# A fused hybrid decoder layer on one core: seven-product groups with one weight sum made by an adding transfer, two made by one VectorE instruction, and five more such groups

## The chip, the cores and the metric

The kernel runs on one core of a Trainium2 chip, as one launch. The metric is device time in microseconds (us), the median of a few runs. Engines are named as in the profile: PE is TensorE (PEld its weight loads), DVE is VectorE, ACT is ScalarE, POOL is GpSimd, SP is SyncE. A "queue" of an engine is the order in which it starts its own instructions, transfers that it issues included.

## The reference

One decoder layer on 256 tokens of width 2048, all in float32: a norm, one wide projection, a state-space scan and an attention (with dilations) side by side, an output projection, a norm, a two-layer MLP with a squared ReLU, a norm. What matters here are the matrix products with W_out (4096 x 2048), W_up (2048 x 8192) and W_down (8192 x 2048):

```python
y_mix = jnp.concatenate([y_ssm, y_att], axis=-1)
mix = jnp.einsum('bse,ed->bsd', y_mix, w_out)
h = h + rmsnorm(mix, norm_mix_post[i])
u = rmsnorm(h, norm_mlp_pre[i])
hdn = jax.nn.relu(jnp.einsum('bsd,df->bsf', u, w_up))
ff = jnp.einsum('bsf,fd->bsd', hdn * hdn, w_down)
h = h + rmsnorm(ff, norm_mlp_post[i])
```

## The kernel before, in words

**Precision by splitting.** The matmuls take a 32-bit type of reduced precision, so each float32 operand is split into two parts (`split`, L138 and L139): ACT copies it into the reduced type (`hi`), and DVE subtracts that from the original (`lo`). A product is then three matmuls: hi by hi, hi by lo, lo by hi. Weights are split as they come in, activations once they exist. In the profile a weight tile is `raw` (or `raw_p`, from another pool), its parts `hi` and `lo` (or `hi_p`, `lo_p`).

**Groups.** From the sixth pair of row blocks of W_out on, the work is a list of groups (`Group`). A group is 256 rows by 1024 columns of a weight matrix, 1 MB: two row blocks of 128 (a with index 0, 1 for the row block and b for the second half of the columns), each a `raw` tile of 128 x 2 x 512. It is multiplied by the matching 256 features of both halves of the tokens. There are four results of 128 tokens by 512 columns, held in four PSUM banks over all the groups of a unit (a unit is a half of W_out, an eighth of W_up, a half of W_down).

A **plain** group (`plain`, L815 to L817) makes eight block products of three matmuls: 24 matmuls of 512 columns. A **seven-product** group (`seven`, L827 to L829) uses the Strassen-Winograd scheme for 2 x 2 blocks: seven block products, 21 matmuls. It needs sums of weight blocks and of activation blocks first, and has four more PSUM banks (`more`), which `combine` adds together after the last seven-product group of a unit (L877 to L881), and `final` joins to the plain ones (L885). The weights' sums are made by `add` (L793, four DVE instructions of 128 x 512, one of them written over a half of raw[0]); three of the results lie in one tile `xr`, which is split into `xh` and `xl` (one tile each, 128 x 1536). The activations' sums are made by `sums` (L707 to L715: tile `uu`, split into `q` or `m` tiles); sums of W_out's and W_up's activations are kept for the next unit, those of W_down are made for each group, since there the activations are the hidden columns. Those are also split again for every two groups (`ready`, q<-m).

**Order.** From here on the program's order is written by hand (a manual schedule): each engine runs its instructions as they were recorded. `run` walks through a unit; before the matmuls of group i, `advance(i + 2)` records work ahead: the fetch of group i + 4 (two 512 KB transfers on SP's queue, L784), the splits of group i + 2 (`divide`), the weight sums and the activation sums of group i + 3. Six raw tiles (three groups) and six pairs of hi and lo (three groups) are in turn, one `xr`, one `xh` and one `xl`. A fetch waits until the tile of the group three earlier is split; a split waits until TensorE is done with the group three earlier. In a seven-product group raw[1] is fetched and split first.

POOL's queue holds in this part only a few transfers of 1 MB (L910: norm weights, L950: x or the stored h, L991: h to memory) and a few small operations.

Of the kernel before, what the change touches and what calls it, by code (L numbers as in the profile page):

```python
# [14 lines left out]
ALU = mybir.AluOpType  # L15

P = 128
# [54 lines left out]
def hymba_layer(ctx: ExitStack, tc: tile.TileContext, x, norm_mix_pre, w_in, conv_w, conv_b, dt_bias, a_log,  # L72
# [604 lines left out]
    class Mix:  # L677
# [32 lines left out]
        def sums(self):  # L710
            if self.k not in self.kept:
                a, c = self.source(), quarters(strip())
                nc.vector.tensor_tensor(c[:, 0:2], a[:, 0::3], a[:, 1:2].to_broadcast([P, 2, P]), op=ALU.subtract)
                nc.vector.tensor_tensor(c[:, 2], a[:, 0], c[:, 1], op=ALU.add)
                nc.vector.tensor_tensor(c[:, 3], a[:, 2], c[:, 2], op=ALU.subtract)  # L715
                d = self.tile()
                split(d[:, 0], d[:, 1], c)
                self.kept[self.k] = d
            self.d = self.kept[self.k]
# [54 lines left out]
    class Group:  # L774
# [3 lines left out]
        def fetch(self):  # L778
            self.raw = [raw_tile() for _ in range(KB)]
            self.hl = [None, None]  # L780
            cs = slice(self.n * NB, (self.n + 2) * NB)
            for j in (1, 0) if self.by_seven else (0, 1):
                k = self.acts.k * KB + j
                nc.sync.dma_start(self.raw[j].rearrange("p b n -> p (b n)"), self.src[k * P:(k + 1) * P, cs])  # L784

        def add(self):
            if not self.by_seven:
                return
            self.x = pp.tile([P, 3, NB], F32, name="xr")
            (a0, b0), (a1, b1) = ((r[:, 0], r[:, 1]) for r in self.raw)  # L790
            e0, s, t4 = (self.x[:, i] for i in range(3))
            for dst, p, q in ((e0, a0, b0), (s, b0, b1), (b0, e0, b1), (t4, b0, a1)):
                nc.vector.tensor_tensor(dst, p, q, op=ALU.add)  # L793

# [4 lines left out]
        def divide(self):  # L799
            self.acts.ready()  # L800
            for j in (1, 0) if self.by_seven else (0, 1):
                if self.hl[j] is None:
                    self.part(j, hl_tiles())
            if self.by_seven:
                self.xhl = aside()
                split(*self.xhl, self.x)
# [12 lines left out]
        def seven(self, acc, more, first, last):  # L819
            block, summed = self.acts.block, self.acts.summed  # L820
            (a0, e1), (a1, b1) = ([[v[:, b] for v in hl] for b in range(2)] for hl in self.hl)
            e0, s, t4 = ([v[:, i] for v in self.xhl] for i in range(3))
            for dst, (a_h, a_l), (hi, lo), own in (
                    (acc[0], block(1, 0), a1, False), (acc[1], summed(3), b1, False),
                    (more[0], block(0, 0), a0, True), (more[2], summed(2), e1, True),
                    (more[1], summed(1), e0, True), (more[3], summed(0), s, True), (acc[2], block(1, 1), t4, False)):
                nc.tensor.matmul(dst, a_h, hi, start=own and first, stop=False)  # L827
                nc.tensor.matmul(dst, a_h, lo, start=False, stop=False)  # L828
                nc.tensor.matmul(dst, a_l, hi, start=False, stop=own and last)  # L829
# [10 lines left out]

    at = {"fetch": 0, "add": 0, "sums": 0, "divide": 0}

    def advance(to, sums=True):

        with tc.high_priority(offset=AHEAD):
            for what, last in (("fetch", to + 2), ("divide", to), ("add", to + 1), ("sums", to + 1)):
                while at[what] <= min(last, len(groups) - 1):
                    g = groups[at[what]]
                    if what == "divide" and at["add"] == at["divide"]:
                        g.add()  # L850
                        at["add"] += 1
                    if what == "sums":
# [20 lines left out]
    def combined(r):  # L873

        def combine(more):
            u_ = strip()
            nc.scalar.activation(r[0, 0], more[0], AF.Copy)  # L877
            nc.vector.tensor_tensor(u_, r[0, 0], more[2], op=ALU.subtract)
            nc.vector.tensor_tensor(r[1, 0], more[3], u_, op=ALU.add)
# [4 lines left out]
    def final(r, acc, t, b):  # L884
        nc.vector.tensor_tensor(r[t, b], acc[b + 2 * t], r[t, b], op=ALU.subtract if b else ALU.add)  # L885

# [21 lines left out]
    def load_wpost(pool, src):  # L908
# [3 lines left out]

    wo0 = plan(w_out, 0, Mix, order_of(range(EARLY, 16), (6, 9, 12)))
    wo1 = plan(w_out, 2, Mix, order_of((0, 1, 6, 2, 4, 3, 9, 5, 12, 7, 8, 10, 11, 13, 14, 15), (6, 4, 9, 12, 8)))
    up = [plan(w_up, 2 * n, Pre,
               order_of(range(8), ()) if n == 0 else
               order_of((0, 1, 3, 2, 5, 4, 7, 6), (3, 5, 7)) if n < 7 else
               order_of((0, 1, 3, 2, 5, 4, 6, 7), (3, 5))) for n in range(8)]
    down = [plan(w_down, 2 * n, Hidden, order_of(range(32), range(4, 27, 3) if n == 0 else range(3, 25, 3)))
            for n in range(2)]  # L920
# [161 lines left out]
    for n in range(8):  # L1082
# [5 lines left out]
        else:  # L1088
            hooks.update({i: Pre(k).sums for i, k in ((0, 3), (1, 5), (2, 7))})
        run(unit, acc, more, combined(r), hooks, started=n == 0)  # L1090
# [65 lines left out]
```

## Time and profile before

| | |
|---|---|
| median of three runs | 1495.16 us (1495.01 to 1495.42) |
| profiled execution, its own time | 1493.86 us |
| its span, first to last instruction | 1491.8 us |
| granted TensorE clock, mean | 0.995 |
| busy: PE, PEld, DVE, ACT, POOL | 1471.1, 1242.0, 1157.7, 845.2, 54.1 us |
| matmuls | 7229 |
| read from memory | 281.78 MB, 192 GB/s over the span |
| seven-product groups (xh splits counted) | 44 |

The kernel runs W_in with its scan and attention until some 603 us, W_out until 789, W_up until 1143 and W_down to the end. Busy shares are means over these stages. In a row of the timeline the first number is the start and the second the duration in us; then come engine, line, operation, the tiles written and read, and in brackets how long the engine sat idle before it and what ended that. Instructions of one engine overlap a little (the next starts before the last has fully ended), so what an instruction costs its engine is the distance from its start to the next one's.

### The profile page before, as it was taken

Reading aid. Unit: us, or ns where it says so; the run is one execution under the profiler, and the core shown is the slowest. Engines: PE = TensorE matmul, PEld = TensorE weight load, DVE = VectorE, ACT = ScalarE, POOL = GpSimd, SP = SyncE. Lnnn points to the kernel's source line nnn. Section 1 sums busy time; section 2 is a strip of 40 time slices with the busy share of each in tenths; the row PEclk is TensorE's granted clock in tenths of the full one; section 3 lists DMA queues with packets and bytes.
Section 4 is the critical chain, followed back from the end, with each engine's and each line's share of the span. In section 5 each row is a group of like instructions: output and inputs, shape, how many; then the busy total and the mean of one; then the engine's idle time right before and its main releaser. Section 6 shows DMA issues by size and latency. Waiting matters only on the chain. (4 is left out here: it accounts for less than half of the span.)

```text
span 1491.8 us, 19561 instructions
## 1 busy us (share of the span) xinstructions
PE 1471.1 (99%) x7229; PEld 1242.0 (83%) x7229; DVE 1157.7 (78%) x1609; ACT 845.2 (57%) x1138; POOL 54.1 (4%) x77
## 2 busy tenths in 40 slices
PE   9999999999999999999997999999999999999997
PEld 8888888888888888878885888888888888888886
DVE  6988897886555555597987778888887899779995
ACT  7574565455545454554556565676665665656462
POOL 0002100220000000000001000000000000000000
PEclk9999999999999999999999999999999999999998
DMA  7666666555656555555674555655555556657652
GB/s 270 203 201 181 182 185 186 182 169 169 175 167 182 169 170 176 190 169 205 247 238 176 187 176 211 211 186 187 197 182 193 199 196 216 221 186 259 219 188 96
DMA packets 108751, 287.28 MB, mean 193 GB/s; under 512 B 11392, under 2 KB 14320, under 8 KB 107632
## 3 DMA queue, kind: packets, MB, share of 16 engines
q1 hardware_dynamic: 103632, 272.37, 56.2%
q0 software_dynamic: 1152, 8.39, 1.6%
q10 hardware_dynamic: 3872, 5.28, 1.1%
q8 instruction: 56, 0.92, 0.3%
q14 instruction: 39, 0.32, 0.1%
HBM read 281.78 MB, written 4.23 MB: 192 GB/s over the span
## 5 line engine op out<-in xcount | busy, mean ns | idle before, releaser
L139 DVE TENSOR_TENSOR lo<-raw,hi 128x1024 fp32r<-128x1024 f32 (+1 forms) x367 | 447.9, 1224 | 181.6 <-ACT hi L138 180.8
L138 ACT ACTIVATE hi<-raw 128x1024 fp32r<-128x1024 f32 (+1 forms) x367 | 383.7, 1050 | 278.1 <-PE acc L221 108.5
L221 PE MATMUL acc<-q,hi 128*128 128x512 f32 x1024 | 283.3, 402 | 0.6 <-DVE q L141 0.6
L221 PEld LDWEIGHTS acc<-q,hi 128*128 128x128 f32 x1024 | 178.8, 189 | 27.3 <-DVE q L141 0.8
L817 PE MATMUL acc<-hi,q 128*128 128x512 f32 x472 | 183.7, 389 | 0.0
L815 PE MATMUL acc<-hi,q 128*128 128x512 f32 x472 | 183.6, 389 | 0.0
L816 PE MATMUL acc<-lo,q 128*128 128x512 f32 x472 | 183.6, 389 | 0.0
L224 PEld LDWEIGHTS acc<-q,lo 128*128 128x128 f32 x1024 | 152.9, 189 | 19.2
L224 PE MATMUL acc<-q,lo 128*128 128x256 f32 x1024 | 157.8, 281 | 0.0
L139 DVE TENSOR_TENSOR lo<-raw_p,hi 128x1024 fp32r<-128x1024 f32 x95 | 115.8, 1219 | 16.3 <-ACT hi L138 16.2
L138 ACT ACTIVATE hi<-raw_p 128x1024 fp32r<-128x1024 f32 x95 | 99.7, 1050 | 33.3 <-DVE raw_p L793 15.0
L816 PEld LDWEIGHTS acc<-lo,q 128*128 128x128 f32 x472 | 88.6, 188 | 18.5
L817 PEld LDWEIGHTS acc<-hi,q 128*128 128x128 f32 x472 | 88.6, 188 | 18.5
L815 PEld LDWEIGHTS acc<-hi,q 128*128 128x128 f32 x472 | 88.6, 188 | 18.3
L199 PE MATMUL acc<-hi,q 128*128 128x512 f32 x256 | 100.1, 391 | 0.0
L200 PE MATMUL acc<-lo,q 128*128 128x512 f32 x256 | 99.7, 389 | 0.0
L201 PE MATMUL acc<-hi,q 128*128 128x512 f32 x256 | 99.7, 389 | 0.0
L138 ACT ACTIVATE q<-uu 128x512 fp32r<-128x512 f32 x21 | 13.3, 632 | 132.9 <-DVE uu L715 132.9
L139 DVE TENSOR_TENSOR xl<-xr,xh 128x1536 fp32r<-128x1536 f32 x44 | 77.3, 1757 | 11.2 <-ACT xh L138 11.0
L138 ACT ACTIVATE xh<-xr 128x1536 fp32r<-128x1536 f32 x44 | 65.1, 1480 | 15.3 <-PE ps L829 7.5
L139 DVE TENSOR_TENSOR lo_p<-raw,hi_p 128x1024 fp32r<-128x1024 f32 x43 | 52.5, 1220 | 12.8 <-ACT hi_p L138 12.8
L815 PE MATMUL ps<-hi,q 128*128 128x512 f32 x152 | 59.5, 392 | 0.0
(361 smaller groups left out, 2565.3 us busy)
## 6 DMA issues: line engine op xcount, KB each, us to landing
raw<-in_w_in_dram SPq DMA_DIRECT2D x190, 512.0 KB, 3.6
raw<-in_w_up_dram SPq DMA_DIRECT2D x86, 512.0 KB, 4.5
raw<-in_w_down_dram SPq DMA_DIRECT2D x85, 512.0 KB, 5.1
raw<-in_w_out_dram SPq DMA_DIRECT2D x46, 512.0 KB, 4.0
raw_p<-in_w_down_dram SPq DMA_DIRECT2D x43, 512.0 KB, 5.1
raw_p<-in_w_up_dram SPq DMA_DIRECT2D x42, 512.0 KB, 4.6
raw_p<-in_w_out_dram SPq DMA_DIRECT2D x18, 512.0 KB, 5.1
bc<-acs_d ACTq DMA_DIRECT2D x8, 512.0 KB, 4.6
```

The lines of the kernel that those rows point to most:

```text
L138: return (nc.scalar.activation(hi, src, AF.Copy), nc.vector.tensor_tensor(lo, src, hi.bitcast(F32), op=ALU.subtract))
L139: nc.vector.tensor_tensor(lo, src, hi.bitcast(F32), op=ALU.subtract))
L199: nc.tensor.matmul(acc[t], a_h[:, r, ts], hi[:, j], start=begin, stop=False)
L200: nc.tensor.matmul(acc[t], a_h[:, r, ts], lo[:, j], start=False, stop=False)
L201: nc.tensor.matmul(acc[t], a_l[:, r, ts], hi[:, j], start=False, stop=end)
L221: nc.tensor.matmul(acc[f], hi[:, j, f * P:(f + 1) * P], u(k0 + j), start=k0 + j == 0, stop=False, skip_group_check=True)
L224: nc.tensor.matmul(acc[f][:, 0], lo[:, j, f * P:(f + 1) * P], u(k0 + j)[:, 0], start=False, stop=k0 + j == NK - 1, skip_group_check=True)
L815: nc.tensor.matmul(a, a_h, hi[:, b], start=first and j == 0, stop=False)
L816: nc.tensor.matmul(a, a_h, lo[:, b], start=False, stop=False)
L817: nc.tensor.matmul(a, a_l, hi[:, b], start=False, stop=last and j == KB - 1)
```

## The change

The seven-product groups get another form of the scheme. With a0, b0 the two halves of row block 0 and a1, b1 those of row block 1, the sum s = b0 + b1 is made by a transfer: POOL issues a third load, of the 256 KB of b1, that adds to the half of raw[0] that holds b0 (L786 of the new kernel). It has to wait until raw[0] has landed. `add` then is two DVE instructions (L793 and L794 of the new kernel): x0 = s - a0 of 128 x 512, and x1, x2 = (a1, b1) - x0 as one of 128 x 1024. It isn't a step of its own one group ahead any more, but stands in `divide` between the splits of raw[1] and raw[0]. The activations' sums and the signs in `combine` and `final` change with the scheme, at the same number and size of instructions. Two products change places in `seven`.

The groups are placed anew. W_out's first half has four seven-product groups instead of three (its groups 1, 3, 5 and 7, counted from 0; before 1, 4 and 7), its second half five as before, W_up twenty as before, at the same places in a unit but with row pair 1 in place of 5. Each half of W_down has ten instead of eight: groups 4, 7, 9, 12, 15, 17, 20, 23, 25, 28 of the first (before every third from 4 to 25) and 3, 6, 8, 11, 14, 16, 19, 22, 24, 27 of the second (before every third from 3 to 24). That makes 49 instead of 44.

```diff
--- before.py
+++ after.py
@@ -710,7 +710,7 @@
         def sums(self):
             if self.k not in self.kept:
                 a, c = self.source(), quarters(strip())
-                nc.vector.tensor_tensor(c[:, 0:2], a[:, 0::3], a[:, 1:2].to_broadcast([P, 2, P]), op=ALU.subtract)
+                nc.vector.tensor_tensor(c[:, 0:2], a[:, 1::2], a[:, 0:2], op=ALU.subtract)
                 nc.vector.tensor_tensor(c[:, 2], a[:, 0], c[:, 1], op=ALU.add)
                 nc.vector.tensor_tensor(c[:, 3], a[:, 2], c[:, 2], op=ALU.subtract)
                 d = self.tile()
@@ -782,15 +782,17 @@
             for j in (1, 0) if self.by_seven else (0, 1):
                 k = self.acts.k * KB + j
                 nc.sync.dma_start(self.raw[j].rearrange("p b n -> p (b n)"), self.src[k * P:(k + 1) * P, cs])
+            if self.by_seven:
+                nc.gpsimd.dma_start(self.raw[0][:, 1], self.src[k * P + P:(k + 2) * P, (self.n + 1) * NB:cs.stop],
+                                    accum_op=ALU.add)
 
         def add(self):
             if not self.by_seven:
                 return
             self.x = pp.tile([P, 3, NB], F32, name="xr")
-            (a0, b0), (a1, b1) = ((r[:, 0], r[:, 1]) for r in self.raw)
-            e0, s, t4 = (self.x[:, i] for i in range(3))
-            for dst, p, q in ((e0, a0, b0), (s, b0, b1), (b0, e0, b1), (t4, b0, a1)):
-                nc.vector.tensor_tensor(dst, p, q, op=ALU.add)
+            nc.vector.tensor_tensor(self.x[:, 0], self.raw[0][:, 1], self.raw[0][:, 0], op=ALU.subtract)
+            nc.vector.tensor_tensor(self.x[:, 1:3], self.raw[1], self.x[:, 0:1].to_broadcast([P, KB, NB]),
+                                    op=ALU.subtract)
 
         def part(self, j, tiles):
             self.hl[j] = tiles
@@ -801,6 +803,8 @@
             for j in (1, 0) if self.by_seven else (0, 1):
                 if self.hl[j] is None:
                     self.part(j, hl_tiles())
+                if j and self.by_seven:
+                    self.add()
             if self.by_seven:
                 self.xhl = aside()
                 split(*self.xhl, self.x)
@@ -818,12 +822,12 @@
 
         def seven(self, acc, more, first, last):
             block, summed = self.acts.block, self.acts.summed
-            (a0, e1), (a1, b1) = ([[v[:, b] for v in hl] for b in range(2)] for hl in self.hl)
-            e0, s, t4 = ([v[:, i] for v in self.xhl] for i in range(3))
+            (a0, s), (a1, b1) = ([[v[:, b] for v in hl] for b in range(2)] for hl in self.hl)
+            x0, x1, x2 = ([v[:, i] for v in self.xhl] for i in range(3))
             for dst, (a_h, a_l), (hi, lo), own in (
                     (acc[0], block(1, 0), a1, False), (acc[1], summed(3), b1, False),
-                    (more[0], block(0, 0), a0, True), (more[2], summed(2), e1, True),
-                    (more[1], summed(1), e0, True), (more[3], summed(0), s, True), (acc[2], block(1, 1), t4, False)):
+                    (more[0], block(0, 0), a0, True), (more[3], summed(0), s, True),
+                    (more[2], summed(2), x0, True), (more[1], summed(1), x2, True), (acc[2], block(1, 1), x1, False)):
                 nc.tensor.matmul(dst, a_h, hi, start=own and first, stop=False)
                 nc.tensor.matmul(dst, a_h, lo, start=False, stop=False)
                 nc.tensor.matmul(dst, a_l, hi, start=False, stop=own and last)
@@ -838,17 +842,14 @@
     def order_of(ks, by_seven):
         return [(k, k in by_seven) for k in ks]
 
-    at = {"fetch": 0, "add": 0, "sums": 0, "divide": 0}
+    at = {"fetch": 0, "sums": 0, "divide": 0}
 
     def advance(to, sums=True):
 
         with tc.high_priority(offset=AHEAD):
-            for what, last in (("fetch", to + 2), ("divide", to), ("add", to + 1), ("sums", to + 1)):
+            for what, last in (("fetch", to + 2), ("divide", to), ("sums", to + 1)):
                 while at[what] <= min(last, len(groups) - 1):
                     g = groups[at[what]]
-                    if what == "divide" and at["add"] == at["divide"]:
-                        g.add()
-                        at["add"] += 1
                     if what == "sums":
                         if g.by_seven:
                             g.acts.sums()
@@ -875,14 +876,14 @@
         def combine(more):
             u_ = strip()
             nc.scalar.activation(r[0, 0], more[0], AF.Copy)
-            nc.vector.tensor_tensor(u_, r[0, 0], more[2], op=ALU.subtract)
+            nc.vector.tensor_tensor(u_, more[2], r[0, 0], op=ALU.add)
             nc.vector.tensor_tensor(r[1, 0], more[3], u_, op=ALU.add)
             nc.vector.tensor_tensor(r[0, 1], more[1], u_, op=ALU.add)
             nc.vector.tensor_tensor(r[1, 1], more[3], r[0, 1], op=ALU.add)
         return combine
 
     def final(r, acc, t, b):
-        nc.vector.tensor_tensor(r[t, b], acc[b + 2 * t], r[t, b], op=ALU.subtract if b else ALU.add)
+        nc.vector.tensor_tensor(r[t, b], acc[b + 2 * t], r[t, b], op=ALU.add)
 
     def four():
         return {(t, b): pp.tile([P, NB], F32, name="r", bufs=4) for t in range(NT) for b in range(2)}
@@ -910,13 +911,14 @@
         nc.gpsimd.dma_start(w.rearrange("p n c -> p (n c)"), src[0].partition_broadcast(P))
         return w
 
-    wo0 = plan(w_out, 0, Mix, order_of(range(EARLY, 16), (6, 9, 12)))
+    wo0 = plan(w_out, 0, Mix, order_of((5, 6, 7, 9, 10, 8, 11, 12, 13, 14, 15), (6, 9, 8, 12)))
     wo1 = plan(w_out, 2, Mix, order_of((0, 1, 6, 2, 4, 3, 9, 5, 12, 7, 8, 10, 11, 13, 14, 15), (6, 4, 9, 12, 8)))
     up = [plan(w_up, 2 * n, Pre,
                order_of(range(8), ()) if n == 0 else
-               order_of((0, 1, 3, 2, 5, 4, 7, 6), (3, 5, 7)) if n < 7 else
-               order_of((0, 1, 3, 2, 5, 4, 6, 7), (3, 5))) for n in range(8)]
-    down = [plan(w_down, 2 * n, Hidden, order_of(range(32), range(4, 27, 3) if n == 0 else range(3, 25, 3)))
+               order_of((0, 2, 3, 4, 1, 5, 7, 6), (3, 1, 7)) if n < 7 else
+               order_of((0, 2, 3, 4, 1, 5, 6, 7), (3, 1))) for n in range(8)]
+    down = [plan(w_down, 2 * n, Hidden, order_of(range(32), (4, 7, 9, 12, 15, 17, 20, 23, 25, 28) if n == 0 else
+                     (3, 6, 8, 11, 14, 16, 19, 22, 24, 27)))
             for n in range(2)]
 
     region = tc.manual_schedule()
@@ -1086,7 +1088,7 @@
         if n:
             hooks[1] = turned
         else:
-            hooks.update({i: Pre(k).sums for i, k in ((0, 3), (1, 5), (2, 7))})
+            hooks.update({i: Pre(k).sums for i, k in ((0, 3), (1, 1), (3, 7))})
         run(unit, acc, more, combined(r), hooks, started=n == 0)
         acc, more = more, acc
```

DVE's instructions in the first half of W_down, from one group's activation sums (q<-uu) to the next one's (uu<-m), before:

```order
L139 TENSOR_TENSOR q<-uu,q 128x512
L139 TENSOR_TENSOR lo<-raw_p,hi 128x1024
L139 TENSOR_TENSOR lo<-raw,hi 128x1024
L139 TENSOR_TENSOR xl<-xr,xh 128x1536
L139 TENSOR_TENSOR q<-m,q 128x1024
L139 TENSOR_TENSOR lo_p<-raw,hi_p 128x1024
L139 TENSOR_TENSOR lo<-raw,hi 128x1024
L139 TENSOR_TENSOR lo<-raw_p,hi 128x1024
L139 TENSOR_TENSOR lo<-raw,hi 128x1024
L793 TENSOR_TENSOR xr<-raw 128x512
L793 TENSOR_TENSOR xr<-raw,raw_p 128x512
L793 TENSOR_TENSOR raw<-xr,raw_p 128x512
```

and the same stretch of the changed kernel, at two seven-product groups that stand two apart:

```order
L139 TENSOR_TENSOR q<-uu,q 128x512
L139 TENSOR_TENSOR lo<-raw,hi 128x1024
L793 TENSOR_TENSOR xr<-raw_p 128x512
L794 TENSOR_TENSOR xr<-raw,xr 128x1024
L139 TENSOR_TENSOR lo<-raw_p,hi 128x1024
L139 TENSOR_TENSOR xl<-xr,xh 128x1536
L139 TENSOR_TENSOR q<-m,q 128x1024
L139 TENSOR_TENSOR lo<-raw,hi 128x1024
L139 TENSOR_TENSOR lo<-raw_p,hi 128x1024
L713 TENSOR_TENSOR uu<-m 128x256
L714 TENSOR_TENSOR uu<-m,uu 128x128
```

The four additions, which stood ahead of the activation sums and so ahead of their group's splits, are gone; two subtractions stand between the two lo of the group itself, and between two groups' sums lie one plain group's lo instead of two.

POOL's queue in W_out's second half, before (L910 is norm_mix_post, L950 x):

```order
L910 DMA m<-in_norm_mix_post_dram 128x2048
L950 DMA m<-in_x_dram 128x2048 x2
L906 TENSOR_TENSOR rmix<-mean,half 128x1
L1000 TENSOR_TENSOR m<-m 128x512
L906 TENSOR_TENSOR rmix<-mean,half 128x1
```

and in the changed kernel, from the first adding transfer on:

```order
L786 DMA raw_p<-in_w_out_dram 128x512
L786 DMA raw<-in_w_out_dram 128x512 x2
L786 DMA raw_p<-in_w_out_dram 128x512 x2
L786 DMA raw<-in_w_out_dram 128x512 x2
L786 DMA raw_p<-in_w_out_dram 128x512
L911 DMA m<-in_norm_mix_post_dram 128x2048
L786 DMA raw<-in_w_out_dram 128x512
L952 DMA m<-in_x_dram 128x2048 x2
```

The adding transfers stand in one queue with the 1 MB loads: the last of W_out waits behind norm_mix_post, and x behind it.

## The prediction

> **What bounds the kernel now.** I read the page's first block and the timeline of TensorE, then the waits, and then the timelines of VectorE and ScalarE in the stretch that gets the new groups.
>
> ```profile
> span 1491.8 us, 19561 instructions
> PE 1471.1 (99%) x7229; PEld 1242.0 (83%) x7229; DVE 1157.7 (78%) x1609; ACT 845.2 (57%) x1138; POOL 54.1 (4%) x77
> ```
>
> TensorE is busy 99% of the span, so fewer matmuls are worth something wherever nothing else holds it up. Its pace comes from the chain of waits:
>
> ```profile
> 857.33 0.23 PE acc L815
> 893.82 0.23 PE acc L817
> ```
>
> Between these two starts lie 161 matmul steps (two seven-product groups of 21 and five plain ones of 24 matmuls, less one), so a step is 36.49/161 = 0.2266 us (the 389 ns of the page are pipelined durations). A plain group takes 24 x 0.2266 = 5.44 us, a seven-product group 4.76 us, and one more seven-product group saves 0.68 us. VectorE, at 78%, looks free. It isn't in the W_down stage:
>
> ```profile
> 1160.00:1280.00 120.00, 120.00 (x531) 99.41 (x530) 111.08 (x124) 74.22 (x79) 0.00 (x0) 1.00 0.59 197
> ACT q L138 <- DVE uu L715: 45.4, 7, 6.5
> DVE q L139 <- ACT q L138: 7.9, 11, 2.2
> DVE lo L139 <- ACT hi L138: 1.0, 4, 0.3
> ```
>
> The first row is a window (PE, PEld, DVE, ACT, POOL busy), the others are the waits of the same 120 us. VectorE is busy 111 of 120 us, its 8.9 us of waits are for ScalarE, and ScalarE waits for VectorE. Neither waits for TensorE or a transfer, so the two run in one closed loop at their own speed:
>
> ```profile
> 1238.84 0.69 DVE L139 TENSOR_TENSOR q<-uu,q 128x512 fp32r<-128x512 f32 x1 [0.70 <-ACT q L138]
> 1239.79 1.22 DVE L139 TENSOR_TENSOR lo<-raw_p,hi 128x1024 fp32r<-128x1024 f32 x1 [0.26 <-ACT hi L138]
> 1240.93 1.22 DVE L139 TENSOR_TENSOR lo<-raw,hi 128x1024 fp32r<-128x1024 f32 x1
> 1242.12 1.76 DVE L139 TENSOR_TENSOR xl<-xr,xh 128x1536 fp32r<-128x1536 f32 x1
> 1243.79 1.22 DVE L139 TENSOR_TENSOR q<-m,q 128x1024 fp32r<-128x1024 f32 x1
> ...
> 1249.47 0.69 DVE L793 TENSOR_TENSOR xr<-raw 128x512 f32<-128x512 f32 x1
> 1250.07 0.69 DVE L793 TENSOR_TENSOR xr<-raw,raw_p 128x512 f32<-128x512 f32 x1
> 1250.79 0.69 DVE L793 TENSOR_TENSOR raw<-xr,raw_p 128x512 f32<-128x512 f32 x1
> 1252.13 0.42 DVE L713 TENSOR_TENSOR uu<-m 128x256 f32<-128x256 f32 x1
> 1252.91 0.29 DVE L715 TENSOR_TENSOR uu<-m,uu 128x128 f32<-128x128 f32 x1
> 1253.90 0.69 DVE L139 TENSOR_TENSOR q<-uu,q 128x512 fp32r<-128x512 f32 x1 [0.70 <-ACT q L138]
> ```
>
> This is one turn of the loop, three groups with one seven-product group. By starts: 0.95 us from q to the first lo, 1.14 a lo, 1.67 the xl, five instructions of 1.14 (four lo and a split of hidden columns, 5.68), 2.66 the four additions, 1.77 the sums of activations with ScalarE's answer. That is 15.06 us; every other turn has one split more, 16.2 us, on average 15.63. TensorE needs 2 x 5.44 + 4.76 = 15.64 us for the same groups. The two are level, and TensorE never waits only because VectorE is a few us ahead.
>
> **The change, part by part.** TensorE: five groups more, 5 x 0.68 = 3.4 us less (one in W_out's first half, two in each half of W_down; W_up keeps its twenty).
>
> VectorE: the four additions (2.66 us) go. In their place, behind the first lo, stand x0 (0.72 us, as 1250.07 to 1250.79, whose successor reads its result) and a two-row subtraction that I price as a lo of the same 1024 elements (1.14; the broadcast operand could make it dearer, and nothing bounds that but the 1.67 of 1536 elements). Then comes the second lo, and xl, which needs ScalarE's xh:
>
> ```profile
> 1240.61 1.48 ACT L138 ACTIVATE xh<-xr 128x1536 fp32r<-128x1536 f32 x1
> ```
>
> xh to xl takes 1.51 us (1240.61 to 1242.12). Before, xh's input was long ready. Now xh can start only when the subtraction has ended (1.22 us and 0.03 after its start), so xl starts 2.77 us after the subtraction, where 1.14 + 1.14 would have been enough: **a new wait of 0.49 us in every seven-product group**, with the next groups' lo queued behind it. A seven-product group now takes of VectorE 0.95 + 1.14 + 0.72 + 1.14 + 1.63 + 1.67 + 1.77 = 9.02 us (before 9.38), a plain one 2.27, a split 1.14 per two groups.
>
> The new order puts two seven-product groups in five. VectorE: 2 x 9.02 + 3 x 2.27 + 2.5 x 1.14 = 27.7 us; TensorE: 3 x 5.44 + 2 x 4.76 = 25.8 us. **VectorE becomes the slower by 1.9 us per five groups.** By steps, TensorE's time less VectorE's: three groups with one split 15.64 - 14.70 = +0.94; with two splits -0.20; two groups 10.20 - 12.43 = -2.23. How far ahead it starts:
>
> ```profile
> 1162.41 1.22 DVE L139 TENSOR_TENSOR lo<-raw_p,hi 128x1024 fp32r<-128x1024 f32 x1
> 1166.69 0.39 PE L827 MATMUL ps<-hi,q 128*128 128x512 f32 x1
> 1325.00 1.23 DVE L139 TENSOR_TENSOR lo_p<-raw,hi_p 128x1024 fp32r<-128x1024 f32 x1 [0.26 <-ACT hi_p L138]
> 1329.89 0.39 PE L827 MATMUL acc<-hi_p,q 128*128 128x512 f32 x1
> 1425.97 2.49 DVE L894 TENSOR_TENSOR r<-r,m 128x512 f32<-128x512 f32 x4
> ```
>
> These are the first lo and the first matmul of the first seven-product group of each half. The lead is 4.28 and 4.89 us; the additions that stood ahead leave, so 6.9 and 7.55. From its first lo a group now needs 1.14 + 0.72 + 1.14 + 1.63 + 1.76 = 6.4 us to the end of xl, which TensorE reads at its 14th matmul, 2.95 us after its first: a lead of 3.5 us is needed (3.7 where a split and a plain group follow).
>
> First half, leads at groups 4, 7, 9, 12, 15, 17, 20, 23, 25: 6.9, 7.8, 5.6, 5.4, 6.3, 4.1, 3.9, 4.8, 2.6. At 25 it is 1.1 short, at 28 just enough: TensorE waits 1.1 us. Second half, at 3, 6, 8, 11, 14, 16, 19, 22: 7.55, 7.35, 5.1, 6.05, 5.85, 3.6, 4.55, 4.35. Before 24 the four weightings (2.41 us, the last row) come too: 4.35 - 2.23 - 2.41 = -0.3, which is 3.8 short; 27 has 4.4. TensorE waits 3.8 us.
>
> W_out's first half has its four such groups two apart, each with the sums' first addition (L707, 0.72 us) on top:
>
> ```profile
> 641.76 0.69 DVE L707 TENSOR_TENSOR uu<-m 128x512 f32<-128x512 f32 x1
> 642.55 0.39 PE L827 MATMUL acc<-hi,m 128*128 128x512 f32 x1
> 644.28 0.50 PE L827 MATMUL acc<-hi,q 128*128 128x512 f32 x1 [0.89 <-ACT q L138]
> ```
>
> TensorE waits there 1.1 us for the sums now; they start some 0.5 us earlier without the additions (saved). Two groups cost VectorE 9.74 + 2.27 = 12.0 against 10.2, 1.8 lost each time: the lead is 5.9 at the second group (sums done about 647.8 against 653.7), then 4.1, then 2.3, which is 1.2 short. So the part saves 0.68 + 0.5 - 1.2, about nothing.
>
> W_up keeps its count, and its first lo of a unit leads enough:
>
> ```profile
> 890.87 1.23 DVE L139 TENSOR_TENSOR lo_p<-raw,hi_p 128x1024 fp32r<-128x1024 f32 x1 [4.45 <-ACT hi_p L138]
> 895.56 0.48 PE L827 MATMUL ps<-hi_p,q 128*128 128x512 f32 x1
> ```
>
> 4.7 us where 3.5 are needed; I price it at nothing, and without that cover each unit would pay.
>
> The adding transfer has no row before. It waits on POOL's queue for raw[0], and x0, ScalarE's second hi and all behind them wait for it. Its tile comes free at the end of the second lo of the group three earlier, 3.0 + 1.22 = 4.2 us after that group's first lo; then:
>
> ```profile
> raw<-in_w_down_dram SPq DMA_DIRECT2D x85, 512.0 KB, 5.1
> raw<-in_w_in_dram SPq DMA_DIRECT2D x4, 256.0 KB, 4.6
> xs<-in_x_dram SPq DMA_DIRECT2D x8, 256.0 KB, 6.6
> m<-in_norm_mix_post_dram POOLq DMA_DIRECT2D x1, 1024.0 KB, 9.3
> 1341.82 0.54 POOL L950 DMA_DIRECT2D m<-hd  x1 [17.32 <-DVE q L139]
> ```
>
> 4.2 + 5.1 to land + 0.54 to issue = 9.8 us; x0 stands at 14.70 + 1.14 = 15.8 us (17.0 with two splits). There is room for 6.0 us. The bounds are 4.6 us (256 KB) and 9.3 us (1 MB on POOL's queue); by size it is nearest the 256 KB rows, so I take 4.6, on time, at no cost. POOL's other transfers wait for nothing new that is needed soon: of norm_mlp_post, hd and x, each is wanted tens of us later. The Trainium skill (DMA: Bandwidth & Descriptors, Anatomy of one DMA) gives for a POOL transfer 2.0 us plus bytes/436e3; that would be an estimated 2.6 us, and the sum would stay; no run here shows it.
>
> **The sum.** W_out 0.0; first half of W_down -1.36 + 1.1 = -0.3; second half -1.36 + 3.8 = +2.4: **+2.1 us**. The profiled execution took 1493.86 us (1491.8 span and 2.1 around it), so 1496.0; the three runs have a median of 1495.16, 1.3 above it, so **1497.2 us**. About 0.2% (3 us) is what a measurement here can tell from no change.
>
> **Rivals.**
>
> *The lead suffices* (20%). The leads are sums over many small steps; 4 us more, for instance if the weightings hide or xh starts sooner, and none of the waits is left: -3.4 - 0.5 = 1491.3 us. For it: TensorE shows no wait after 815 us now, and VectorE's work falls by 0.8 us per group by durations. Against it: the loop has no slack in its rows.
>
> *The adding transfer is late* (27%), and the kernel slower. Place: x0 in W_down, from 6.0 us of landing. At 6.6 us each of the three groups per half that follow a seven three earlier with one split is 0.6 late; leads fall by 1.8 per half, and with half of that at the two-split groups by some 2.5, nearly all paid at the end: +5, 1502. At 9.3 us it is 3.3 and 2.1 us on three each, 16 us per half, about 1528. For it: the transfer reads its destination too, and the DMA share is already 0.59. The Trainium skill (SBUF — State Buffer, The "DVE blocks DMA" trap, under SBUF: two separate sides) says that VectorE in its two-port modes keeps POOL from writing descriptors; the same page excepts tensor_tensor, which is all that VectorE runs here, so it gives no time.
>
> *A wait of TensorE drops its clock* (8%):
>
> ```profile
> 809.01 0.79 PE L815 MATMUL ps<-hi_p,q 128*128 128x512 f32 x1 [4.48 <-ACT hi_p L138]
> 811.29 0.63 PE L815 MATMUL acc<-hi_p,q 128*128 128x512 f32 x1
> 811.72 0.63 PE L816 MATMUL acc<-lo_p,q 128*128 128x512 f32 x1
> ```
>
> After 4.5 us of idling the steps were 0.43 us. If the 3.8 us of the second half fell in one piece, another 3 to 4 us would go: 1501. I expect it in three pieces (first lo, second lo, xl).
>
> **Chances.** Forecast 45%, its own range 1494 to 1500.5. Faster by over 0.2%: 0.15, three quarters of the first rival. Slower by over 0.2%: 0.40, the second and third rival and the edge of the forecast. Within: 0.45. The range runs from the first rival's 1491.3 to 1504, between the late transfer at 6.6 us and that at 9.3.
>
> **What would show it.** Right: xl waits about 0.5 us for xh in each group; the waits list TensorE waiting for lo or xl late in both halves of W_down, most after the weightings; twice 25.8 us of matmuls take longer there. Wrong: no such waits (first rival); x0 waiting for a DMA (second); matmul steps of 0.43 us in W_down (third).

## The result and the profile after

| | before | changed |
|---|---|---|
| median of 4 runs | 1495.1 us | 1512.28 us |
| ratio, 95% interval | 1 | 1.0114 (1.0097 to 1.0132) |
| profiled execution, span | 1491.8 us | 1510.3 us |
| W_out and the first unit of W_up | 213.5 us | 215.8 us |
| the rest of W_up | 305.1 us | 305.0 us |
| W_down to the last matmul | 326.3 us | 340.8 us |

The stages are measured on TensorE: from the first matmul of the written-out order to the first transposition of `turned` (the function that turns the finished hidden columns of W_up around for W_down), from there to the last one, and on to the last matmul. W_up is as it was. W_out is 2.3 us longer and W_down 14.5 us, although each of W_down's four new groups saves 0.68 us of matmuls: TensorE waits there 16.8 us (the sum of what its steps over 0.25 us have beyond 0.2266 us), and 0.1 before. Of the rest of the difference between the two profiles 1.6 us lie ahead of the 49th us of the kernel, where nothing was changed; all profiles of this study scatter by that much there (they reach the first matmul of the table at 636.7 to 638.7 us).

The page of the changed kernel, its first block:

```profile
span 1510.3 us, 19655 instructions
PE 1475.7 (98%) x7214; PEld 1237.3 (82%) x7214; DVE 1151.5 (76%) x1552; ACT 857.2 (57%) x1147; POOL 96.8 (6%) x126
```

VectorE has 6 us less to do in all than before (1157.7) and the kernel is slower: the sum of its work did not grow. The waits of the stretch 1158 to 1490 us, W_down (engine, line, what is waited for: us in total, times, longest):

```profile
DVE xl L139 <- ACT xh L138: 9.9, 20, 0.5
DVE xr L793 <- DMA raw<-in_w_down_dram: 4.7, 5, 2.2
PEld ps L832 <- DVE xl L139: 4.5, 5, 1.0
PEld acc L820 <- DVE lo L139: 4.1, 6, 1.6
PEld acc L832 <- DVE xl L139: 3.3, 4, 1.0
PEld ps L832 <- DVE lo L139: 2.9, 3, 1.8
DVE xr L793 <- DMA raw_p<-in_w_down_dram: 2.6, 3, 1.4
```

Two kinds of wait are new. xl waits 0.50 us for xh in each of the 20 groups, as forecast. And x0 (L793) waits for a transfer, 7.3 us in all; that one had been priced at nothing. The page's block of transfers says why (KB each, and the median us from issue to landing):

```profile
raw<-in_w_down_dram POOLq DMA_DIRECT2D x14, 256.0 KB, 6.5
raw<-in_w_up_dram POOLq DMA_DIRECT2D x13, 256.0 KB, 4.2
raw_p<-in_w_up_dram POOLq DMA_DIRECT2D x7, 256.0 KB, 4.1
raw_p<-in_w_down_dram POOLq DMA_DIRECT2D x6, 256.0 KB, 7.2
```

The adding transfer takes 4.2 us in W_up, but 6.9 us (median of 20; 4.1 to 8.7) in W_down. A landing is counted from the start of the issue, so these figures contain the 0.87 us for which GpSimd is busy issuing it. One case in the timelines of SyncE, GpSimd, VectorE and TensorE, the group with index 28 of the first half, three behind that with index 25:

```profile
1282.62 0.33 SPq L784 DMA_DIRECT2D raw<-in_w_down_dram  x1
1289.01 0.87 POOL L786 DMA_DIRECT2D raw<-in_w_down_dram  x1 [16.62 <-DMA raw<-in_w_down_dram]
1294.31 1.22 DVE L139 TENSOR_TENSOR lo<-raw_p,hi 128x1024 fp32r<-128x1024 f32 x1
1297.76 0.69 DVE L793 TENSOR_TENSOR xr<-raw 128x512 f32<-128x512 f32 x1 [2.23 <-DMA raw<-in_w_down_dram]
1298.48 1.22 DVE L794 TENSOR_TENSOR xr<-raw_p,xr 128x1024 f32<-128x1024 f32 x1
1299.62 1.22 DVE L139 TENSOR_TENSOR lo<-raw,hi 128x1024 fp32r<-128x1024 f32 x1
1300.90 0.50 PE L832 MATMUL acc<-lo,q 128*128 128x512 f32 x1 [1.19 <-DVE lo L139]
```

The tile comes free and is loaded from 1282.62 us on, GpSimd issues the addition at 1289.01, and x0 starts when it has landed, 8.7 us later, after an idle 2.23 us. The second lo stands behind x0 on VectorE and TensorE waits for it. The order of these events is the one that the prediction worked out, with room for the landing: x0 was due 1.14 us after the start of the lo ahead of it, at 1295.45, 6.4 us after the issue. Only the landing was priced at 4.6.

In W_out the same happens twice, and with the longest waits of x0 in the kernel, at its last two seven-product groups (rows of VectorE, then of TensorE):

```profile
735.15 0.69 DVE L793 TENSOR_TENSOR xr<-raw_p 128x512 f32<-128x512 f32 x1 [3.15 <-issue]
749.43 0.69 DVE L793 TENSOR_TENSOR xr<-raw 128x512 f32<-128x512 f32 x1 [5.53 <-issue]
752.57 0.50 PE L832 MATMUL acc<-lo,m 128*128 128x512 f32 x1 [0.70 <-DVE lo L139]
754.83 0.50 PE L832 MATMUL acc<-xl,q 128*128 128x512 f32 x1 [0.58 <-DVE xl L139]
```

The view gives no releaser for these two ("issue"), but each x0 starts 0.08 us after its adding transfer has landed. The second one's raw[0] took 9.8 us to load, while the 1 MB of norm_mix_post were on their way, and its addition landed 8.0 us after its issue. GpSimd issued it as soon as raw[0] had landed; that it stands behind norm_mix_post in the queue cost nothing.

### The profile page after: what moved, and what is told of

Read it like the earlier page. It is cut to its first block, busy times and chain, and to the rows that moved or that the text cites. A ratio compares the mean times of both kernels' runs of the same rounds, so it can differ in the third digit from the quotient of the medians.

```text
span 1510.3 us, 19655 instructions
## 1 busy us (share of the span) xinstructions
PE 1475.7 (98%) x7214; PEld 1237.3 (82%) x7214; DVE 1151.5 (76%) x1552; ACT 857.2 (57%) x1147; POOL 96.8 (6%) x126
## 5 line engine op out<-in xcount | busy, mean ns | idle before, releaser
L820 PE MATMUL acc<-lo,q 128*128 128x512 f32 x438 | 171.1, 391 | 1.7 <-DVE lo L139 1.7
L821 PE MATMUL acc<-hi,q 128*128 128x512 f32 x438 | 170.5, 389 | 0.0
L819 PE MATMUL acc<-hi,q 128*128 128x512 f32 x438 | 170.5, 389 | 0.0
L138 ACT ACTIVATE xh<-xr 128x1536 fp32r<-128x1536 f32 x49 | 73.0, 1491 | 80.8 <-DVE xr L794 76.5
L139 DVE TENSOR_TENSOR xl<-xr,xh 128x1536 fp32r<-128x1536 f32 x49 | 86.2, 1758 | 24.1 <-ACT xh L138 24.1
L199 PE MATMUL acc<-hi,q 128*128 128x512 f32 x256 | 100.1, 391 | 0.0
L200 PE MATMUL acc<-lo,q 128*128 128x512 f32 x256 | 99.7, 389 | 0.0
L201 PE MATMUL acc<-hi,q 128*128 128x512 f32 x256 | 99.7, 389 | 0.0
L820 PEld LDWEIGHTS acc<-lo,q 128*128 128x128 f32 x438 | 82.2, 188 | 21.1 <-DVE lo L139 4.1
L819 PEld LDWEIGHTS acc<-hi,q 128*128 128x128 f32 x438 | 82.2, 188 | 17.2
L821 PEld LDWEIGHTS acc<-hi,q 128*128 128x128 f32 x438 | 82.2, 188 | 16.8
```

The costliest lines, as they stand in the source:

```text
L138: return (nc.scalar.activation(hi, src, AF.Copy), nc.vector.tensor_tensor(lo, src, hi.bitcast(F32), op=ALU.subtract))
L139: nc.vector.tensor_tensor(lo, src, hi.bitcast(F32), op=ALU.subtract))
L199: nc.tensor.matmul(acc[t], a_h[:, r, ts], hi[:, j], start=begin, stop=False)
L200: nc.tensor.matmul(acc[t], a_h[:, r, ts], lo[:, j], start=False, stop=False)
L201: nc.tensor.matmul(acc[t], a_l[:, r, ts], hi[:, j], start=False, stop=end)
L819: nc.tensor.matmul(a, a_h, hi[:, b], start=first and j == 0, stop=False)
```

## The experiments

Theory A: the adding transfer is late. Theory B: VectorE's own work at three seven-product groups in eight (with xl's wait) is too much. Each ratio is to the runs of the kernel before beside it, with its 95% interval.

| kernel | median us | ratio | W_out part | W_down |
|---|---|---|---|---|
| before | 1495.1 | 1 | 213.5 | 326.3 |
| changed | 1512.3 | 1.0114 (1.0097 to 1.0132) | 215.8 | 340.8 |
| without the adding transfers | 1500.2 | 1.0038 (1.0023 to 1.0053) | 213.4 | 332.5 |
| new form, old placement | 1496.1 | 1.0010 (1.0001 to 1.0020) | 213.8 | 328.2 |
| old form, new placement | 1509.3 | 1.0096 (1.0079 to 1.0113) | 218.0 | 337.3 |
| sum by a GpSimd instruction | 1521.4 | 1.0180 (1.0164 to 1.0195) | 215.7 | 349.3 |
| raw[0] loaded ahead of raw[1] | 1503.7 | 1.0060 (1.0045 to 1.0075) | 214.5 | 334.6 |
| half of raw[0] loaded first | 1504.2 | 1.0063 (1.0046 to 1.0079) | 215.5 | 334.2 |
| without transfers, x first | 1491.0 | 0.9975 (0.9966 to 0.9984) | 211.6 | 323.6 |
| old form, 48 groups, late split | 1492.1 | 0.9979 (0.9970 to 0.9989) | 213.3 | 323.6 |
| raw[0] first and x first | 1500.9 | 1.0043 (1.0030 to 1.0055) | 212.4 | 334.4 |
| new form, 49 groups, all edits | 1490.8 | 0.9976 (0.9963 to 0.9989) | 211.6 | 323.6 |

The last two columns are the stages of the first table, in each kernel's profile. W_down without any wait is 326.3 - 0.1 - 4 x 0.68 = 323.5 us.

### Without the adding transfers

```
-            if self.by_seven:
-                nc.gpsimd.dma_start(self.raw[0][:, 1], ..., accum_op=ALU.add)
```

> The changed kernel without the 49 adding transfers: x0 is computed from b0 instead of b0+b1, so the seven-product groups give wrong sums, while every other instruction stays. It leaves out the sum of weights. Theory A, the adding transfer is late: in W_down the transfers land 6 to 8.7 us after their issue, x0 waits for 9 of 20 of them, 7.3 us in all, and that lateness is what TensorE pays at last. Then x0 waits for no transfer, TensorE's waits in W_down fall from 16.8 us to about 7.5 (the 4.9 of the forecast and some 2.6 at the three late groups, which were not priced), and the time is about 1502. Theory B, VectorE's own work at three seven-product groups in eight: the wait of xl and the spacing use the lead up, the transfers only fill time that VectorE would wait anyway. Then the time stays within 2 us of 1512.

1500.2 us: **12.1 of the 17 us belong to the transfer.** W_down is 8.3 us shorter than with it, W_out's part 2.4 us; the two profiles differ by another 2 us ahead of the table's first matmul, where all profiles scatter. What is left in W_down, 8.6 us of waits, is theory B's part: 1.9 us in the first half, 4.5 in the second up to its last seven-product group, and 2.2 us in the three late groups. The rows of that last piece stand at the same place in the changed kernel (TensorE's timeline there):

```profile
1484.38 0.50 PE L820 MATMUL acc<-lo_p,q 128*128 128x512 f32 x1 [1.23 <-DVE lo_p L139]
1485.52 0.50 PE L820 MATMUL acc<-lo,q 128*128 128x512 f32 x1 [0.17 <-DVE lo L139]
1486.65 0.50 PE L820 MATMUL acc<-lo,q 128*128 128x512 f32 x1 [0.16 <-DVE lo L139]
1487.79 0.50 PE L820 MATMUL acc<-lo,q 128*128 128x512 f32 x1 [0.17 <-DVE lo L139]
```

The three late groups are multiplied a quarter of their products at a time, so TensorE runs through all three sets of weights in 18 matmuls, 4.1 us, where VectorE needs six lo, 6.8 us. The last seven-product group now stands at index 27, four places from the end (24 before), and the four combining instructions come behind it.

### Form and placement apart

Two kernels: the new form with the old placement (below), and the old form (the code of before, with its four additions and no adding transfer) with the lists of the change.

```
-    wo0, up, down: the lists of the change
+    wo0, up, down: the lists of before
```

> The new form with the old placement (44 seven-product groups, three groups apart in W_down). Theory A: most transfers in W_down are still some 0.3 to 1.4 us late for x0, but VectorE has 0.37 us per three groups to spare (15.27 against 15.64) and starts 7 us ahead, so the lateness comes out of the lead: TensorE waits little, 1495 to 1498. Theory B: nothing waits, 1494.5 to 1495.5. Either way most of the 17 us is gone, so it isn't the form alone; if it stays above 1503, the form alone is the cause.

> The old form (four additions on VectorE, no adding transfer) with the new placement of 49 groups. Theory B: VectorE needs 3 x 9.38 + 5 x 2.27 + 4 x 1.14 = 44.05 us for eight groups in W_down where TensorE needs 41.5, 2.55 us lost per eight; a lead of 4.3 to 4.9 us with 1.2 needed is used up by group 15 or so: some 5 us of waits per half and 2.4 more after the weightings, less the 3.4 us of matmuls saved: about 1503, and above 1508 if B explains all of the loss. Theory A: here there is no late transfer, so no more than that 1503.

The new form in the old places costs 0.1%, 1.5 us: small, and just clear of nothing. In W_down its transfers are late almost every time:

```profile
DVE xr L793 <- DMA raw<-in_w_down_dram: 9.3, 11, 1.3
```

11 of 16 wait, 9.3 us in all, and TensorE waits 1.8 us in W_down. All groups there are three apart, and VectorE has the time. So the late transfer was there at once; the new placement made it cost something.

The old form in the new places came out 6 us above the 1503 expected. TensorE waits 13.4 us in W_down, where 12.4 had been worked out (twice 5 and 2.4), 2.6 of them in the late groups: VectorE's load is real. The piece that was missed is in W_out, 4.5 us longer than before, where TensorE's second group waits for the sums of activations behind the four additions:

```profile
647.71 0.80 PE L827 MATMUL acc<-hi,q 128*128 128x512 f32 x1 [3.52 <-ACT q L138]
648.30 0.63 PE L828 MATMUL acc<-lo,q 128*128 128x512 f32 x1
648.73 0.63 PE L829 MATMUL acc<-hi,q 128*128 128x512 f32 x1
649.15 0.63 PE L827 MATMUL ps<-hi,m 128*128 128x512 f32 x1
```

3.5 us of waiting, and then matmul steps of 0.43 us instead of 0.23 for 5 us (the granted clock there is 0.50): the prediction's third rival, seen here and not in the W_down of the changed kernel.

### The chain: tile, load, adding transfer

In `fetch`, raw[0] first (the adding transfer's source is written anew, so that it stays the same rows; left out here):

```
-            for j in (1, 0) if self.by_seven else (0, 1):
+            for j in (0, 1):
```

And, for the seven-product groups, half of raw[0] first:

```
-                nc.sync.dma_start(self.raw[j] ...)
+                nc.sync.dma_start(self.raw[0][:, 1], ...)
+                nc.sync.dma_start(self.raw[1], ...)
+                nc.sync.dma_start(self.raw[0][:, 0], ...)
```

> The changed kernel, where the two loads of a seven-product group are issued in the other order: raw[0], on which the adding transfer waits, ahead of raw[1]. Theory A (chain): what is late is a chain of tile free, load (4 to 6 us), issue on GpSimd's queue (0.9) and adding transfer (7 us median in W_down), so anything that starts it earlier pays. For seven-product groups three apart raw[0]'s tile is the one that comes free last, 1.14 us after the other, so little is won there; for the others 1.1 us. x0's waits in W_down fall from 7.3 us to 4 to 6, the time from 1512 to 1508 to 1511. Theory A2 (contention): the transfer is slow because the loads of the next groups are issued 0.3 to 1 us ahead of it and share the DMA engines; then its landing stays 7 us whatever the order and the time stays at 1511 to 1513.

> The changed kernel, where raw[0] of a seven-product group is loaded in two transfers: its half b0 first, then raw[1], then its half a0. The adding transfer needs only b0 and can start earlier by what 256 KB land sooner than 512 KB and raw[1]. Theory A (chain): issue some 1 to 3 us earlier, x0's waits in W_down fall from 7.3 to under 3 us, the time to 1504 to 1508. Theory A2 (contention): the adding transfer then runs beside raw[1] and a0 and lands later after its issue (8 to 9 us), so that x0 is no earlier: 1510 to 1514.

Both give most of what leaving the transfer out gave: 8.6 and 8.1 of 12.1 us. With raw[0] first x0 waits in W_down fall to a fifth:

```profile
DVE xr L793 <- DMA raw<-in_w_down_dram: 0.8, 1, 0.8
DVE xr L793 <- DMA raw_p<-in_w_down_dram: 0.8, 2, 0.6
```

That is more than the 1.1 us of an earlier issue was expected to do (1508 to 1511). The load of raw[0] itself landed sooner, in 3.8 us instead of 5.3 (medians in W_down), and the addition's landing got shorter too, against A2: 6.3 us in W_down instead of 6.9, and 4.2 in W_out instead of 5.9. So what was late was a chain, and one load that nobody was waiting for yet stood in it. Loading half of raw[0] first does no better: the landing falls to 4.9 us, x0's waits to 1.4 us, and W_down is as long as with raw[0] first.

Why a landing takes 4 or 8 us is not settled by a run. In the trace of the changed kernel the 12 adding transfers beside which at most two loads were on their way landed in 3.9 to 4.2 us, and the 36 with four or more in 3.9 to 8.7, median 6.3. That is a coincidence in one trace, not a test; in the kernel with the new form in the old places one with two loads beside it took 7.6 us.

### VectorE's order

In `divide`, x0 and the two-row subtraction ahead of both lo, at first in the kernel without the adding transfers:

```
+            if self.by_seven:
+                self.add()
             for j in (1, 0) ...:
                 self.part(j, hl_tiles())
-                if j and self.by_seven:
-                    self.add()
```

> The kernel without the adding transfers (the sum of weights is left out, x0 computed from b0) with the two subtractions ahead of the first lo instead of between the two lo. ScalarE can then make xh while VectorE works on both lo. Theory B for what is left of the loss (VectorE's load): the wait of xl for xh, 0.50 us in every one of 20 groups of W_down, goes; three seven-product groups in eight then take 3 x 8.53 + 5 x 2.27 + 4 x 1.14 = 41.5 us of VectorE, as many as TensorE needs, and the lead of 7 us holds. The waits of W_down (1.2 and 5.7 us without the transfer) and most of the 1.4 us in W_out go: 1500.2 - 7 = about 1493, below the kernel before. If the wait of xl is only time that VectorE has to spare, 1500.

1491.0 us, 9.2 less than without the edit, and W_down at 323.6 has no wait left: theory B's remainder was the 0.50 us of xl in each group, and the late groups' wait went with it. The bounds of the sum were thus right: 49 groups can save their 3.4 us if neither xl nor a transfer is waited for.

With the transfer in place:

> The changed kernel with both edits that helped one side each: raw[0] loaded ahead of raw[1], and the two subtractions ahead of the first lo. By VectorE's load alone (theory B) the 9.2 us that the second edit gave without transfers come off the 1503.7 of the first: 1494.5. By the chain of theory A the second edit has a price here: x0 stands 1.14 us earlier, so between the x0 of two groups three apart lie 4.2 us to the end of the second lo, 5.2 of load, 0.9 of issue and 6.3 of transfer and some 0.3 between, 16.9 us, where TensorE needs 15.6; x0 waits for the transfer again in most groups of W_down, 8 to 15 us in all, of which the lead covers about half: 1496 to 1501.

1500.9 us, at the upper end of what the chain said. The landing took 7.2 us (median in W_down), where 6.3 and 0.9 for the issue had been put in, though a landing contains its issue: the two errors cancel. The waits of VectorE in W_down:

```profile
DVE xr L793 <- DMA raw<-in_w_down_dram: 9.5, 6, 2.2
DVE xr L793 <- DMA raw_p<-in_w_down_dram: 6.6, 4, 2.0
```

xl waits for nothing any more (9.9 us gained), x0 waits 16.1 us instead of 1.6 (14.5 lost; 8 to 15 had been expected), and W_down is as long as without the edit, 334.4 against 334.6 us. The 2.8 us that are gained are in W_out and ahead of it. **Here an engine that came sooner to a wait only waited longer there.**

### The sum on GpSimd

```
-                nc.gpsimd.dma_start(self.raw[0][:, 1], ..., accum_op=ALU.add)
+                nc.gpsimd.tensor_tensor(self.raw[0][:, 1], self.raw[0][:, 1], self.raw[1][:, 1], op=ALU.add)
```

> The changed kernel with the sum b0+b1 as one GpSimd addition (128x512) in place of the adding transfer, in the same place on its queue. A GpSimd product of this size took 1.27 us before, against 4 to 8.7 us of landing. Theory A: x0 waits for nothing, the time equals that of the kernel without the sum (about 1502). Theory B: 1510 to 1513. If GpSimd's addition slows VectorE's instructions where they overlap, VectorE's lo and x0 get longer than 1.14 and 0.72 us and the time lies above the kernel without the sum by that much times 49.

The worst kernel of all, 1521.4 us, though x0 waits for no transfer. The timelines of GpSimd and VectorE:

```profile
1200.40 1.22 DVE L139 TENSOR_TENSOR lo<-raw_p,hi 128x1024 fp32r<-128x1024 f32 x1
1201.07 1.69 POOL L786 TENSOR_TENSOR raw_p<-raw_p,raw 128x512 f32<-128x512 f32 x1 [17.00 <-DMA raw_p<-in_w_down_dram]
1201.54 2.31 DVE L139 TENSOR_TENSOR lo_p<-raw,hi_p 128x1024 fp32r<-128x1024 f32 x1
1203.77 1.21 DVE L139 TENSOR_TENSOR lo<-raw,hi 128x1024 fp32r<-128x1024 f32 x1
```

The lo that runs beside the addition takes 2.31 us instead of 1.22. Over W_out, W_up and W_down 40 lo that overlap one by 0.3 us or more take 1.85 us on average, the 270 that overlap none 1.22. In W_down VectorE's instructions are 16 us longer by this in all, and the stage is 16.8 us longer than in the kernel without the transfers. The Trainium skill (SBUF — State Buffer, Who interferes with whom) says that a VectorE instruction with two inputs in SBUF contends with a GpSimd instruction that reads SBUF; this trace agrees, with 0.6 us per overlap.

### Two kernels that are faster

The first keeps the old form and takes the new placement in W_up and W_down (48 groups); the split of the sums of activations is put behind the next group's lo (in W_out it stays where it was):

```
-                split(d[:, 0], d[:, 1], c)
+                due.append((d[:, 0], d[:, 1], c))
...
             for j in (1, 0) ...:
                 self.part(j, hl_tiles())
+            settle()
```

> The old form (no adding transfer) with the new placement in W_up and W_down and the old one in W_out, 48 seven-product groups, and one edit of VectorE's order: in W_up and W_down the split of the sums of activations (ScalarE's rounding and VectorE's remainder) is issued behind the next group's two lo, not straight behind the sums. So VectorE no longer waits 0.70 us for ScalarE's q and 0.26 us for the hi behind it. Theory B: a seven-product group then takes 9.38 - 0.96 = 8.4 us of VectorE, three in eight 41.2 us against TensorE's 41.5, no wait of TensorE in W_down, and the four more groups save 2.7 us: 1492 (1490.5 to 1494). If the old form at the new placement lost its time to something else than VectorE's load (1509 with 49 groups), it stays above 1500.

1492.1 us, the forecast of its expectation. W_down has no wait left, 323.6 us where the old form at the same places took 337.3: what held it up there was VectorE, with its waits for ScalarE. The wait for ScalarE's q at the sums is gone, 11.2 us in the kernel before (first row) and 0.0 here (second row; a group's busy us, mean ns, then idle time before it):

```profile
L139 DVE TENSOR_TENSOR q<-uu,q 128x512 fp32r<-128x512 f32 x16 | 11.1, 693 | 11.2 <-ACT q L138 11.2
```
```profile
L139 DVE TENSOR_TENSOR q<-uu,q 128x512 fp32r<-128x512 f32 x20 | 13.7, 683 | 0.0
```

The second takes the new form with all 49 groups, raw[0] loaded first, x0 and the subtraction first, then the lo of raw[0] (so that its tile comes free 1.14 us sooner; TensorE starts with a0), and the late split in W_up and W_down:

> The new form with 49 groups and every edit: raw[0] loaded ahead of raw[1], the subtractions first, then the lo of raw[0] and then that of raw[1] (TensorE takes the product of a0 first), and in W_up and W_down the split of the sums of activations behind both lo. The chain from x0 to x0 three groups later becomes 3.0 us to the end of raw[0]'s lo, 0.3, 5.2, 0.9 and 6.3: 15.7 us, level with TensorE's 15.6, and VectorE needs 8.53 - 0.96 = 7.6 us for a seven-product group, far under what TensorE takes. Theories A and B together: no wait of TensorE in W_down beyond 1 us, x0 waiting for transfers in most groups at no cost, and the 3.4 us of matmuls saved: 1491 (1490 to 1493). If a third cause holds TensorE up, above 1494.

1490.8 us, 0.9976 of the kernel before (0.9963 to 0.9989). Its page, and two of VectorE's waits in W_down:

```profile
span 1486.8 us, 19696 instructions
PE 1466.7 (99%) x7214; PEld 1238.2 (83%) x7214; DVE 1145.9 (77%) x1552; ACT 859.6 (58%) x1147; POOL 96.8 (7%) x126
```
```profile
DVE xr L802 <- DMA raw<-in_w_down_dram: 8.1, 5, 2.1
DVE xr L802 <- DMA raw_p<-in_w_down_dram: 3.0, 3, 2.2
```

x0 still waits 11 us for transfers, more than in the changed kernel, and W_down has no wait of TensorE left (323.6 us). The same wait that cost 8 us there costs nothing here: VectorE comes early enough to make up for it. From a group's first lo, which stands behind x0 here, to its first matmul there are still 5.8 to 9.2 us in W_down (0.5 to 7.9 in the changed kernel, whose x0 comes behind that lo). Against the 1500.9 us above two edits are new here, the order of the two lo and the late split; no run takes them apart. Between the two fast kernels lie 1.3 us, less than their intervals tell apart.

## Why the prediction was wrong

The forecast was +2.1 us and 1497.2; measured are 17 us and 1512.3, outside the range. By its steps:

1. **The step that failed is the price of the adding transfer: "so I take 4.6, on time, at no cost".** It landed after 6.9 us (median in W_down); x0 waited in 8 of 20 groups there (the waits view), all of them three behind another seven-product group, as the rival had it. The choice between the bounds 4.6 and 9.3 was made by the size of the transfer. The rows of the same 256 KB that the prediction had quoted went from 4.6 to 6.6 us, the room was 6.0, and of the two the lower was taken. The room itself was right: 5.7 to 7.8 us from the issue to when x0 was due, at the twelve groups that stand three behind another (forecast 6.0, or 7.2 with two splits). Some luck is in that: the 0.54 us for the issue is part of a landing, but GpSimd started 0.56 to 0.69 us after raw[0] had landed, for which the sum had no term. The late transfers cost 8.2 us in W_down (16.8 us of waits with, 8.6 without) and 2.4 in W_out, where the prediction had not looked for them.
2. **The rival had the place and the mechanism, and a price too low**: 1502 at 6.6 us, where 1512 was measured at 6.9. It counted three groups per half with 0.6 us each and some 2.5 us per half. Landings scatter from 4.1 to 8.7, so single groups were 0.2 to 2.2 us late, 7.3 us in all, and TensorE paid all of it (8.2 us more of waits than without the transfers), for its lead was already spent by theory B. The late groups and W_out came on top.
3. **The late groups were not priced**: 2.2 us without the transfer, 2.9 with it. The sum stopped at the last seven-product group, as if any lead would do behind it.
4. **The waits from VectorE's load were right in place and 1.5 us too low.** Forecast 1.1 us in the first half and 3.8 in the second up to its last seven-product group; the kernel without transfers shows 1.9 and 4.5. The leads (first matmul less first lo) of the first half there are 6.9, 7.9, 5.6, 5.3, 6.1, 3.8, 3.7, 4.6, 2.2, forecast 6.9, 7.8, 5.6, 5.4, 6.3, 4.1, 3.9, 4.8, 2.6. 1497.2 with these 1.5 us and the 2.2 of the late groups is 1500.9; that kernel took 1500.2.
5. xl's wait: 0.49 forecast, 0.50 in each group. The two-row subtraction costs what a lo costs, 1.14 us from its start to the next one's; its broadcast operand adds nothing. The wait for xl is what used the lead up, as the edit of VectorE's order showed (9.2 us without transfers).
6. W_out's three terms cancel as forecast when no transfer is late (213.4 against 213.5 us). W_up was rightly priced at nothing: 305.0 against 305.1, although x0 waits there too, 8.2 us in six groups, more than in W_down. It is the lead that differs: 9.6 us or more at these six groups. The same lateness costs nothing where the lead covers it.
7. The first rival (the lead suffices) did not hold in the changed kernel. Its time was 1491.3; 1491.0 was measured with both waits of VectorE taken away, and 1490.8 with the lead made so long that x0's wait didn't matter. The third (steps of 0.43 us after a wait) is not seen in W_down.

## What to carry to other kernels

Price a transfer of a kind that the trace does not show at the upper end of its size's rows, and add up its whole chain: the tile's last reader, the load, the issue, the landing, against the due time of the instruction that waits; if the room lies inside the spread of the landings, some will be late, and the lead decides who pays. Where an engine level with TensorE gets a new wait, ask first for the order in which its instructions and the loads stand: here the order of two loads was worth 8.6 us, and that of a subtraction and a lo 9.2 without transfers and nothing in W_down with them. And count the lead to the very end of a stage: work that is consumed in a burst there needs more of it than the steady turns.

## What the hardware showed that was not expected

The same adding transfer of 256 KB landed in 3.9 us and in 8.7, in one kernel. A GpSimd addition of 128x512 made the VectorE instruction beside it half again as long (1.22 to 1.85 us on average, 2.3 at worst), and took 1.29 to 2.23 us itself, where the GpSimd product in the kernel before took 1.27.
